# A streaming encoder layer on one core: down projections behind the next gate, reordered block products, low parts on GpSimd, modulation in smaller doses

## The chip, the cores and the metric

The kernel runs on one core of one Trainium2 chip. The metric is the time of one execution on the device, in microseconds (us); lower is better. Five engines work side by side, each through a queue of its own that it takes strictly in order: TensorE (PE, with its weight loads shown apart as PEld), VectorE (DVE), ScalarE (ACT), GpSimd (POOL) and SyncE (SP), which here issues the DMA transfers. Semaphores order work between engines.

## The reference

One layer of a streaming encoder for 1024 prompt frames and 32 sample frames, in fp32:

```python
def swiglu(h, w_gate, w_up, w_down):
    return (jax.nn.silu(h @ w_gate) * (h @ w_up)) @ w_down

mod = jax.nn.silu(c) @ w_mod + b_mod          # nine vectors: shift, scale, gate of three sub-layers
sh1, sc1, g1, sh2, sc2, g2, sh3, sc3, g3 = jnp.split(mod, N_MOD, axis=-1)
h = adaln_in(x, gains[0], sh1, sc1)
x = x + FFN_RES * g1[:, None] * rmsnorm(swiglu(h, w1_gate, w1_up, w1_down), gains[1])
h = adaln_in(x, gains[2], sh2, sc2)
...
x = x + g2[:, None] * rmsnorm(o, gains[3])
h = adaln_in(x, gains[4], sh3, sc3)
x = x + FFN_RES * g3[:, None] * rmsnorm(swiglu(h, w2_gate, w2_up, w2_down), gains[5])
```

The model width is 1024, the inner width of each SwiGLU (FFN1, FFN2) 2816. Between them stand one combined projection, two attention mixers and an output projection.

## The kernel before

The 1056 tokens are three blocks, `tb` 0, 1 and 2, of 384, 384 and 288. Each FFN goes through the 2816 inner columns in 11 groups of 256. A round of a group has three steps: gate "g" and up "u" (a 1024 x 256 weight matrix against the tokens), and down "d" (256 x 1024), whose result is added to an accumulator `facc` on VectorE (L802; the first round copies instead, L800). Which blocks a round has is set by `ROUNDS`: FFN1 has eight rounds with all blocks, then three with blocks 0 and 1, then three with block 2 alone; FFN2 has two rounds with blocks 0 and 1, two with block 2, then nine with all.

An fp32 operand is split into a high and a low part. `pair_of` does it for a weight tile `w` of 128x512: ScalarE copies the high part (L539), VectorE subtracts to get the low part (L540). A product then is three matmuls for each slice of 128: high x high, high x low, low x high (`product`, L597). So the first two matmuls need only the high part of the weight, the third the low part.

For blocks 0 and 1 gate and up use a Strassen scheme (`strassen`) of seven products. The weights enter as quarters A11 to A22 and as four sums S1 to S4, which GpSimd makes from the loaded tiles `raw` (`ws<-raw`, L563); the tokens enter as T1 to T4, combined once at the start of the FFN. The table `STRASSEN` sets the order of the products and, for each, the weights, the tokens, the PSUM bank, and whether block 2's plain product with the same quarter follows. The banks are added up on VectorE (L742) as they come; `made` then takes a finished quarter of the result: for gate, SiLU into `sl` on ScalarE; for up, `sl` times the result (L695) on VectorE, and the split of the product into `gg` (high part on ScalarE, L696, low part on VectorE, L697). The down step reads `gg`. PSUM tiles: `gu` holds banks "b" and "d", `ge` banks "a" and "e", `g2` (with `g` and `g_N` forms in the trace) block 2's. Round 0 of an FFN is done without Strassen (`plain`, tiles `gate` and `up`), and so are rounds with block 2 alone.

The list `stages` sets the program order of the steps: "g", "u", "d" of a round, except that among consecutive rounds of block 2 alone, the down step of one is held until behind the gate of the next. `load` and `ready` bring in the weights of the next step and make its first split while the present one runs.

Work that belongs to other parts runs beside the FFN in small steps: `step(n)` takes n steps from a list of generators. In FFN1 that is the modulation for the later sub-layers (`mod_aside`: chunks of three columns, 10 steps each: DMA loads `wma`, products with `csil` on VectorE into `macc`, L248 and L250, a transposition `pmt` on PE, L256, a sum, L257) and the rows of the attention bias. `step` is called with `PACE` = 2 after each Strassen product, with 1 after each pair of down tiles. At the end of the FFN the norm of the next sub-layer runs there: sums of squares `pss` on PE (L374) of `sq` from GpSimd (L387), `pr` (L422), and the normed tokens `h`, which the first projection `pv` reads (L934 to L936).

Weight buffers are few: four or five `raw` tiles, four `w` tiles, five tiles on GpSimd's side. Within a queue, the order of instructions is decided when the program is built: a scheduler with a timeline of its own may let an instruction pass others of its engine that wait.

Of the kernel before, what the change touches and what calls it, by code (L numbers as in the profile page):

```python
# [35 lines left out]
PACE = 2  # L36
# [45 lines left out]
def encoder_step(ctx: ExitStack, tc, x_prompt, x_sample, cache_a_k, cache_a_v, cache_b_k, cache_b_v,  # L82
# [453 lines left out]
    def pair_of(src, tag="w", at=None):  # L536

        w = at if at is not None else t_tile(tag, [128, 2, 4, 128], "w", F32R)
        ae.activation(w[:, 0], src, AF.Copy)  # L539
        ve.tensor_tensor(w[:, 1], src, w[:, 0], op=OP.subtract)  # L540
        return w[:, 0], w[:, 1]

    class Mat:
# [22 lines left out]
        def split(self, name):  # L566
            if name not in self.done:
                self.done[name] = pair_of(self.of(name), *(self.places.pop(0) if self.places else ()))
            return self.done[name]
# [68 lines left out]
    def rounds(key):  # L638
        lead, lag = ROUNDS[key]
        both, n, out = (0, 1, 2), NF // 2, []  # L640
        if lead:
# [5 lines left out]
    STRASSEN = [("A11", "B11", "a", 2), ("S2", "T2", "b", 0), ("S1", "T1", "d", 0), ("S3", "T3", "b", 0),  # L647
                ("A22", "T4", "e", 2), ("S4", "B22", "d", 0), ("A12", "B21", "a", 2), ("A21", None, None, 2)]

    def ffn(key, H, tags, F, facc, wg, wu, wd, per_group, key_out, after, beside=lambda: None):  # L650
# [3 lines left out]
        T, sl, gs, loaded = {}, {}, {}, {}  # L654
        stages = []
        for r, (gi, blocks) in enumerate(plan):
            held = [stages.pop()] if r and blocks == plan[r - 1][1] == (2,) else []
            stages += [(r, "g"), *held, (r, "u"), (r, "d")]
# [43 lines left out]
        def plain(r, what, m, tb, beside):  # L702
            w = TB[tb][1]
            names = [f"A{f + 1}{d + 1}" for f in range(2) for d in range(2)]
            for n, name in enumerate(names):
# [8 lines left out]
                if d == 1:  # L714
                    step(FAST if r == 0 else PACE)
                    made(r, what, f, tb, ps[:, :w])

        def strassen(r, what, m, two, beside):
# [26 lines left out]
            for n, (name, x, at, blk2) in enumerate(seq):  # L745
# [9 lines left out]
                if name == "A11":  # L755
                    ae.activation(temp("s", 1, 0), banks["a"], AF.Copy)
                elif name == "S2":
# [5 lines left out]
                elif name == "A22":  # L763
                    plus(v["s"], "e", "s")
                    made(r, what, 1, 0, v["s"])
                elif name == "S4":
                    plus(v["u"], "d", "u")
                    made(r, what, 0, 1, v["u"])
                elif name == "A12":
                    made(r, what, 0, 0, banks["a"])  # L770
                    if two:
                        made(r, what, 0, 2, banks["0"])
                elif name == "A21":
                    made(r, what, 1, 2, banks["1"])
                step(PACE)

# [36 lines left out]
        for i, (r, what) in enumerate(stages):  # L813
# [12 lines left out]
            if what == "d":  # L826
                for q in range(2):
                    m.split(q, 0)
                order = [tb for tb in (1, 0, 2) if tb in blocks]
# [796 lines left out]
```

## Time and profile before

| | us |
|---|---|
| three runs | 2378.19, 2384.40, 2382.83 |
| their median | 2382.83 |
| the profiled execution | 2381.55 |
| its span in the trace | 2379.7 |
| PE busy | 2158.8 (91%) |
| VectorE busy | 1583.0 (67%) |
| ScalarE busy | 849.1 (36%) |
| GpSimd busy | 440.5 (19%) |

The granted TensorE clock was 0.945 of full on average. The profile's page gives busy time by engine, the costliest groups of instructions by source line, and the DMA queues; the trace behind it can be asked for the waits of an engine, for groups in a window of time, and for the busy time of every engine in given windows. In the trace "out<-in" names what an instruction writes and reads, and L597 is line 597 of the kernel. "dn<-gg" are the down projections, "gu", "ge", "g" and "g2" the products of gate and up, "dn <- ACT gg" in a list of waits says that a down matmul waited for ScalarE's `gg`.

In time: 0 to 139 us the start with round 0 of FFN1; to 848 rounds 1 to 10; to 942 FFN1's last rounds (block 2 alone) and the change to the mixers; to 1513 projections, attention and output projection; to 1709 the first rounds of FFN2; to 2320 its nine full rounds but the last; to 2380 the end.

### The profile page before, as it was taken

The page shows a single profiled execution, that of the slowest core. Times are in us where ns is not written, and L with a number is a line of the kernel's source. Part 1 is how long each engine was busy: PE and PEld are TensorE (multiplying, and loading weights), DVE is VectorE, ACT ScalarE, POOL GpSimd, SP SyncE. Part 2 cuts the span into 40 slices and gives each one's busy share as a digit, 9 for nine tenths or more (in the row PEclk, how much of TensorE's full clock was granted, in tenths as well). Part 3 has the DMA queues.
Part 4 walks back from the last instruction along what each step waited for, and adds up shares of the span by engine and source line. Part 5 has one row for each costly group of instructions (what it writes and reads, how often), then busy time and mean ns, then how long its engine had stood idle before and what let it go on. Part 6 is the DMA issues. An engine that isn't in the chain of part 4 may idle for free.

```text
span 2379.7 us, 34693 instructions
## 1 busy us (share of the span) xinstructions
PE 2158.8 (91%) x13532; PEld 2036.6 (86%) x13532; DVE 1583.0 (67%) x3077; ACT 849.1 (36%) x1814; POOL 440.5 (19%) x449
## 2 busy tenths in 40 slices
PE   7898898799998896999999899948999999999998
PEld 4788798799998896988888589848999999999997
DVE  5899999965566588477544765776655545555548
ACT  4421222122222244367544662523322322222224
POOL 2321111110122023100100413332111102211101
PEclk8899999899999997999999899969999999999999
DMA  8233443331122254110211211311311111111104
GB/s 320 64 113 107 147 126 93 119 107 36 45 63 60 72 169 146 40 39 24 63 28 31 70 54 54 134 57 54 107 54 53 43 39 45 45 45 54 52 29 128
DMA packets 150840, 186.09 MB, mean 78 GB/s; under 512 B 7980, under 2 KB 134356, under 8 KB 149524
## 3 DMA queue, kind: packets, MB, share of 16 engines
q1 hardware_dynamic: 150676, 183.87, 24.8%
q8 instruction: 107, 1.75, 0.3%
q14 instruction: 57, 0.47, 0.1%
HBM read 164.12 MB, written 22.86 MB: 79 GB/s over the span
## 4 chain that ended last, share of the span: by engine, by line
PE 72%; DVE 19%; issue 3%; DMA 3%; ACT 1%; POOL 1%; SPq 0%; DVEq 0%; ACTq 0%; POOLq 0%
PE gu L597 11%; PE ge L597 8%; PE dn L795 6%; PE g L597 6%; PE dn L796 6%; PE dn L797 6%; DVE macc L250 4%; DVE w L540 3%; PE gate L597 3%; PE po L978 2%; PE S L1017 2%; PE pq L342 2%; DVE sl L695 2%; PE pq L344 2%; PE pq L343 2%
## 5 line engine op out<-in xcount | busy, mean ns | idle before, releaser
L795 PE MATMUL dn<-gg,w 128*128 128x384 f32 (+1 forms) x1008 | 344.7, 346 | 96.5 <-ACT gg L696 46.2
L539 ACT ACTIVATE w<-raw 128x512 fp32r<-128x512 f32 x298 | 186.1, 630 | 615.7 <-PE dn L797 226.4
L796 PE MATMUL dn<-gg,w 128*128 128x384 f32 (+1 forms) x1008 | 343.2, 341 | 11.1 <-DVE gg L697 11.1
L802 DVE TENSOR_TENSOR facc<-dn,facc 128x768 f32<-128x768 f32 (+1 forms) x240 | 212.8, 888 | 196.3 <-PE dn L797 194.8
L797 PE MATMUL dn<-gg,w 128*128 128x384 f32 (+1 forms) x1008 | 338.9, 336 | 0.0
L540 DVE TENSOR_TENSOR w<-raw,w 128x512 fp32r<-128x512 f32 x298 | 220.9, 745 | 161.3 <-ACT w L539 160.4
L795 PEld LDWEIGHTS dn<-gg,w 128*128 128x128 f32 x1008 | 199.5, 200 | 109.2 <-ACT gg L696 51.7
L563 POOL TENSOR_TENSOR ws<-raw 128x512 f32<-128x512 f32 x80 | 125.2, 1567 | 827.1 <-DMA raw<-in_w_gate_dram 266.5
L597 PE MATMUL gu<-t,w 128*128 128x384 f32 x1440 | 264.7, 335 | 0.0
L597 PEld LDWEIGHTS gu<-t,w 128*128 128x128 f32 x1440 | 248.6, 188 | 0.3 <-issue 0.2
L597 PE MATMUL g<-h_hi,w 128*128 128x288 f32 x1024 | 232.2, 300 | 18.1 <-DVE sl L695 9.7
L796 PEld LDWEIGHTS dn<-gg,w 128*128 128x128 f32 x1008 | 201.2, 200 | 17.6 <-DVE gg L697 17.4
L797 PEld LDWEIGHTS dn<-gg,w 128*128 128x128 f32 x1008 | 201.3, 200 | 0.0
L597 PEld LDWEIGHTS g<-h_hi,w 128*128 128x128 f32 x1024 | 175.9, 191 | 23.3 <-ACT w L539 12.0
L597 PE MATMUL ge<-h,w 128*128 128x384 f32 x960 | 194.4, 337 | 1.3 <-DVE w L540 0.9
L540 DVE TENSOR_TENSOR w<-ws,w 128x512 fp32r<-128x512 f32 x160 | 117.2, 739 | 82.8 <-ACT w L539 79.9
L539 ACT ACTIVATE w<-ws 128x512 fp32r<-128x512 f32 x160 | 98.9, 627 | 205.7 <-PE dn L797 117.8
L597 PEld LDWEIGHTS ge<-h,w 128*128 128x128 f32 x960 | 167.4, 188 | 1.9 <-DVE w L540 1.3
L250 DVE SCALAR_TENSOR_TENSOR macc<-wma,csil,macc 128x384 f32<-128x384 f32 (+1 forms) x266 | 165.1, 661 | 1.0 <-DMA wma<-in_w_mod_dram 1.0
L597 PE MATMUL g<-h_lo,w 128*128 128x288 f32 x512 | 152.5, 298 | 0.0
L597 PE MATMUL ge<-t,w 128*128 128x384 f32 x480 | 97.5, 341 | 7.3 <-DVE w L540 7.3
L597 PEld LDWEIGHTS g<-h_lo,w 128*128 128x128 f32 x512 | 97.4, 190 | 0.0
(294 smaller groups left out, 4342.0 us busy)
## 6 DMA issues: line engine op xcount, KB each, us to landing
raw<-in_w_gate_dram SPq DMA_DIRECT2D x54, 512.0 KB, 3.9
raw<-in_w_up_dram SPq DMA_DIRECT2D x54, 512.0 KB, 4.2
raw<-in_w_down_dram SPq DMA_DIRECT2D x54, 512.0 KB, 3.6
wma<-in_w_mod_dram SPq DMA_DIRECT2D x72, 384.0 KB, 3.6
raw<-in_w_in_dram SPq DMA_DIRECT2D x18, 512.0 KB, 4.7
raw<-in_w_out_dram SPq DMA_DIRECT2D x13, 512.0 KB, 3.7
wm<-in_w_mod_dram SPq DMA_DIRECT2D x8, 768.0 KB, 9.3
xr<-xs SPq DMA_DIRECT2D x16, 384.0 KB, 4.4
```

What stands on the lines that cost most here:

```text
L250: ve.scalar_tensor_tensor(acc[j], r[:, kk], c, acc[j], op0=OP.mult, op1=OP.add)
L342: te.matmul(ps, w[:, 0, k], hi, start=start, stop=False)
L343: te.matmul(ps, w[:, 0, k], lo, start=False, stop=False)
L344: te.matmul(ps, w[:, 1, k], hi, start=False, stop=stop)
L539: ae.activation(w[:, 0], src, AF.Copy)
L540: ve.tensor_tensor(w[:, 1], src, w[:, 0], op=OP.subtract)
L563: (ge if name in SUMS_POOL else ve).tensor_tensor(a[name], x, y, op=op)
L597: te.matmul(ps, w[a][:, k, :], x[b][k], start=first and k == 0 and q == 0, stop=last and k == n - 1 and q == 2, skip_group_check=True)
L795: te.matmul(ps[:, s, :w], h[:, k % 4, :], g[:, 0, :w], start=q == 0, stop=False)
L796: te.matmul(ps[:, s, :w], h[:, k % 4, :], g[:, 1, :w], start=False, stop=False)
L797: te.matmul(ps[:, s, :w], l[:, k % 4, :], g[:, 0, :w], start=False, stop=q == 1)
L802: ve.tensor_tensor(o, ps[:, :, :w], o, op=OP.add)
```

## The change

1. `PACE` is 1 in FFN1 and stays 2 in FFN2 (`pace`). In `plain`, `step` now stands behind `made` and is called after each product.
2. `pair_of` takes an engine: the low parts of S1 to S4 are made on GpSimd. 160 instructions leave VectorE for GpSimd; every other count of instructions stays.
3. The table `STRASSEN` has a new order: A12 comes second, S4 last. A down step works through the blocks in order 0, 1, 2 instead of 1, 0, 2. Both finished quarters of block 2 are taken after A21.
4. From round 1 on, every round's down step is held until behind the next round's gate, in all rounds and not just in those of block 2 alone. Only round 0's down and the last one follow their own up step.

Lines behind 568 move by one, behind 647 by two.

```diff
--- before.py
+++ after.py
@@ -33,7 +33,7 @@
              (16, 22, 26), (23, 31, 27), (32, 45, 28), (46, 63, 29), (64, 90, 30), (91, 127, 31)]
 
 
-PACE = 2
+PACE = 1
 FAST = 10
 OUTSTEP = 6
 ABREAST = 1
@@ -533,11 +533,11 @@
         yield from norm_h(f, tb, j + 1, H)
 
 
-    def pair_of(src, tag="w", at=None):
+    def pair_of(src, tag="w", at=None, by=None):
 
         w = at if at is not None else t_tile(tag, [128, 2, 4, 128], "w", F32R)
         ae.activation(w[:, 0], src, AF.Copy)
-        ve.tensor_tensor(w[:, 1], src, w[:, 0], op=OP.subtract)
+        (by or ve).tensor_tensor(w[:, 1], src, w[:, 0], op=OP.subtract)
         return w[:, 0], w[:, 1]
 
     class Mat:
@@ -565,7 +565,8 @@
 
         def split(self, name):
             if name not in self.done:
-                self.done[name] = pair_of(self.of(name), *(self.places.pop(0) if self.places else ()))
+                self.done[name] = pair_of(self.of(name), *(self.places.pop(0) if self.places else ()),
+                                          by=ge if name[0] == "S" else ve)
             return self.done[name]
 
     class Rows:
@@ -644,17 +645,18 @@
         out += [(g, (0, 1)) for g in range(n - lag, n)] + [(g, (2,)) for g in range(n - lag, n)]
         return out
 
-    STRASSEN = [("A11", "B11", "a", 2), ("S2", "T2", "b", 0), ("S1", "T1", "d", 0), ("S3", "T3", "b", 0),
-                ("A22", "T4", "e", 2), ("S4", "B22", "d", 0), ("A12", "B21", "a", 2), ("A21", None, None, 2)]
+    STRASSEN = [("A11", "B11", "a", 2), ("A12", "B21", "a", 2), ("S2", "T2", "b", 0), ("S1", "T1", "d", 0),
+                ("S3", "T3", "b", 0), ("A22", "T4", "e", 2), ("A21", None, None, 2), ("S4", "B22", "d", 0)]
 
     def ffn(key, H, tags, F, facc, wg, wu, wd, per_group, key_out, after, beside=lambda: None):
         plan = rounds(key)
         begun = set()
         final = {tb: max(i for i, (g, t) in enumerate(plan) if tb in t) for tb in range(3)}
         T, sl, gs, loaded = {}, {}, {}, {}
+        pace = PACE if key == "h1" else 2
         stages = []
         for r, (gi, blocks) in enumerate(plan):
-            held = [stages.pop()] if r and blocks == plan[r - 1][1] == (2,) else []
+            held = [stages.pop()] if r > 1 else []
             stages += [(r, "g"), *held, (r, "u"), (r, "d")]
 
         def load(i):
@@ -712,8 +714,8 @@
                 product(ps[:, :w], w_, half(tb, d), d == 0, d == 1)
                 beside(n)
                 if d == 1:
-                    step(FAST if r == 0 else PACE)
                     made(r, what, f, tb, ps[:, :w])
+                step((FAST if r == 0 else 3) if d else 2 * (r > 0))
 
         def strassen(r, what, m, two, beside):
             w, w2 = 384, TB[2][1]
@@ -754,6 +756,8 @@
                 beside(n)
                 if name == "A11":
                     ae.activation(temp("s", 1, 0), banks["a"], AF.Copy)
+                elif name == "A12":
+                    made(r, what, 0, 0, banks["a"])
                 elif name == "S2":
                     plus(temp("u", 0, 1), "b", "s")
                 elif name == "S3":
@@ -766,13 +770,10 @@
                 elif name == "S4":
                     plus(v["u"], "d", "u")
                     made(r, what, 0, 1, v["u"])
-                elif name == "A12":
-                    made(r, what, 0, 0, banks["a"])
-                    if two:
-                        made(r, what, 0, 2, banks["0"])
                 elif name == "A21":
+                    made(r, what, 0, 2, banks["0"])
                     made(r, what, 1, 2, banks["1"])
-                step(PACE)
+                step(pace)
 
         owns = {}
 
@@ -826,7 +827,7 @@
             if what == "d":
                 for q in range(2):
                     m.split(q, 0)
-                order = [tb for tb in (1, 0, 2) if tb in blocks]
+                order = list(blocks)
                 ending = any(r == final[tb] for tb in order)
                 todo = [(tb, mp) for tb in order for mp in range(4)] if ending else \
                     [(tb, mp) for h in range(2) for tb in order for mp in (2 * h, 2 * h + 1)]
```

Three places in the order of the queues. First PE in a steady group of FFN2, at the start of a down step. Before (`g2_17531` is block 2's product of the up step; `gg_17662` and `gg_17603` are the `gg` of this same up step):

```order
L597 MATMUL g2_17531<-h_hi_14934,w_17666 128x288 x2
L597 MATMUL g2_17531<-h_lo_14935,w_17666 128x288
L597 MATMUL g2_17531<-h_hi_14934,w_17666 128x288 x2
L597 MATMUL g2_17531<-h_lo_14935,w_17666 128x288
L597 MATMUL g2_17531<-h_hi_14934,w_17666 128x288
L795 MATMUL dn_17717<-gg_17662,w_17655 128x384
L795 MATMUL dn_17741<-gg_17662,w_17655 128x384
L796 MATMUL dn_17717<-gg_17662,w_17655 128x384
L797 MATMUL dn_17717<-gg_17662,w_17655 128x384
L795 MATMUL dn_17717<-gg_17603,w_17658 128x384
```

After (`gu_18366` is S4, the last product of the next round's gate; `gg_18156` and `gg_18252` were made in the previous round's up step, a whole gate step earlier):

```order
L598 MATMUL g2_18315<-h_hi_14938,w_18423 128x288 x2
L598 MATMUL g2_18315<-h_lo_14939,w_18423 128x288
L598 MATMUL g2_18315<-h_hi_14938,w_18423 128x288
L598 MATMUL gu_18366<-h_14562,w_18453 128x384 x12
L796 MATMUL dn_18486<-gg_18156,w_18413 128x384
L797 MATMUL dn_18486<-gg_18156,w_18413 128x384
L798 MATMUL dn_18486<-gg_18156,w_18413 128x384
L796 MATMUL dn_18486<-gg_18252,w_18416 128x384
```

The first down matmul used to stand right behind the up step that makes its `gg`; now a gate step stands between.

Second, GpSimd at the same stage. Before, its queue holds only sums, four for each gate or up step (each `ws` is one of S1 to S4, each pair of `raw` one weight matrix):

```order
L563 TENSOR_TENSOR ws_18021<-raw_17933,raw_17935 128x512
L563 TENSOR_TENSOR ws_18023<-ws_18021,raw_17933 128x512
L563 TENSOR_TENSOR ws_18025<-raw_17935,ws_18023 128x512
L563 TENSOR_TENSOR ws_18147<-raw_17933 128x512
L563 TENSOR_TENSOR ws_18446<-raw_18310,raw_18312 128x512
L563 TENSOR_TENSOR ws_18448<-ws_18446,raw_18310 128x512
L563 TENSOR_TENSOR ws_18450<-raw_18312,ws_18448 128x512
```

After (the `w` rows are low parts; `ws_18636` and the three behind it are the sums of the next up step, from the loads `raw_18500` and `raw_18502`; `w_18453` is the low part of S4 of the gate, which the PE rows above read):

```order
L540 TENSOR_TENSOR w_18334<-ws_18247,w_18334 128x512
L540 TENSOR_TENSOR w_18363<-ws_18245,w_18363 128x512
L540 TENSOR_TENSOR w_18383<-ws_18381,w_18383 128x512
L563 TENSOR_TENSOR ws_18636<-raw_18500,raw_18502 128x512
L563 TENSOR_TENSOR ws_18638<-ws_18636,raw_18500 128x512
L563 TENSOR_TENSOR ws_18640<-raw_18502,ws_18638 128x512
L563 TENSOR_TENSOR ws_18757<-raw_18500 128x512
L540 TENSOR_TENSOR w_18453<-ws_18249,w_18453 128x512
```

The low part `w_18453` stands behind the four sums of the next step, and the first of these waits for the DMA of its two `raw` tiles.

Third, PE at the end of FFN1 (`dn_8132` the last down tile of block 2, `pss_7617` and `pr_7722` the norm of block 0; `h_7743` is block 0's normed tokens). Before:

```order
L795 MATMUL dn_8132<-gg_8072,wd_8057 128x288
L796 MATMUL dn_8132<-gg_8072,wd_8057 128x288
L797 MATMUL dn_8132<-gg_8072,wd_8057 128x288
L374 MATMUL pss_7617<-ones_101,sq_7657 128x1 x3
L374 MATMUL pss_7617<-ones_101,sq_7683 128x1 x3
L422 MATMUL pr_7722<-ident_99,ry_7710 128x128 x3
L934 MATMUL pv_8213<-w_8172,h_7743 128x256
L935 MATMUL pv_8213<-w_8172,h_7743 128x256
L934 MATMUL pv_8268<-w_8172,h_7743 128x256
```

After (`h_7357` is block 0's):

```order
L796 MATMUL dn_8132<-gg_8072,wd_8057 128x288
L797 MATMUL dn_8132<-gg_8072,wd_8057 128x288
L798 MATMUL dn_8132<-gg_8072,wd_8057 128x288
L935 MATMUL pv_8213<-w_8172,h_7357 128x256
L935 MATMUL pv_8268<-w_8172,h_7357 128x256
L935 MATMUL pv_8301<-w_8172,h_7357 128x256
L936 MATMUL pv_8213<-w_8172,h_7357 128x256
L937 MATMUL pv_8213<-w_8172,h_7357 128x256
```

The rows of `pss` and `pr` that stood between the last down tile and the first `pv` are gone from there: block 0's norm is earlier in the queue, and that of block 1 stands some 30 rows behind the first `pv`.

## The prediction

> **What bounds the kernel now.** First the page: busy time by engine, and the costliest groups (operation, tiles, count | busy us, mean ns | idle just before, and what ended it).
>
> ```profile
> PE 2158.8 (91%) x13532; PEld 2036.6 (86%) x13532; DVE 1583.0 (67%) x3077; ACT 849.1 (36%) x1814; POOL 440.5 (19%) x449
> ...
> L540 DVE TENSOR_TENSOR w<-raw,w 128x512 fp32r<-128x512 f32 x298 | 220.9, 745 | 161.3 <-ACT w L539 160.4
> ...
> L563 POOL TENSOR_TENSOR ws<-raw 128x512 f32<-128x512 f32 x80 | 125.2, 1567 | 827.1 <-DMA raw<-in_w_gate_dram 266.5
> ...
> L540 DVE TENSOR_TENSOR w<-ws,w 128x512 fp32r<-128x512 f32 x160 | 117.2, 739 | 82.8 <-ACT w L539 79.9
> L539 ACT ACTIVATE w<-ws 128x512 fp32r<-128x512 f32 x160 | 98.9, 627 | 205.7 <-PE dn L797 117.8
> ```
>
> PE is busy 91% of the 2379.7 us span. The matmul count doesn't change, so what can be won is PE's idle time and the stretches at a lower clock: 221 us of span are not PE-busy. Second view, busy time by stage (columns: length, PE, PEld, DVE, ACT, POOL, granted clock, DMA share, GB/s):
>
> ```profile
> 139.00:848.00 709.00, 642.27 (x3811) 628.00 (x3810) 535.02 (x926) 179.66 (x327) 118.72 (x80) 0.96 0.30 91
> 848.00:942.00 94.00, 71.91 (x496) 70.07 (x495) 84.10 (x151) 47.07 (x76) 24.65 (x17) 0.85 0.55 174
> 942.00:1513.00 571.00, 552.70 (x3894) 478.70 (x3894) 349.04 (x998) 307.40 (x827) 100.15 (x210) 0.97 0.17 51
> 1513.00:1625.00 112.00, 69.01 (x353) 66.55 (x354) 85.67 (x162) 39.79 (x77) 40.74 (x30) 0.79 0.21 73
> 1709.00:2320.00 611.00, 585.56 (x3542) 576.47 (x3543) 327.86 (x464) 161.17 (x300) 105.31 (x71) 0.97 0.15 46
> ```
>
> 139–848 is FFN1 after its first round, 848–942 its end, 942–1513 projections and attention (untouched code), 1513–1709 the start of FFN2, 1709–2320 its steady groups. Third view, single groups: a group with modulation, one without, two rounds without block 2; then two FFN2 groups.
>
> ```profile
> 368.20:452.50 84.30, 74.20 (x432) 71.91 (x432) 78.79 (x146) 18.68 (x34) 12.62 (x9) 0.93 0.39 117
> 594.90:662.20 67.30, 65.78 (x408) 64.93 (x408) 37.54 (x55) 18.19 (x35) 11.54 (x8) 1.00 0.16 48
> 722.20:776.40 54.20, 47.64 (x264) 47.09 (x264) 32.10 (x45) 15.68 (x29) 11.90 (x8) 0.94 0.20 59
> 1756.87:1826.14 69.27, 66.04 (x408) 64.97 (x409) 38.36 (x55) 18.26 (x34) 12.20 (x9) 1.00 0.15 46
> 1826.14:1897.57 71.43, 68.36 (x408) 67.21 (x409) 38.49 (x55) 18.25 (x34) 12.20 (x9) 0.95 0.16 45
> ```
>
> The same group costs 67.3 or 84.3 us by whether VectorE carries modulation (78.8 of 84.3 us busy): early FFN1 is VectorE-bound, everything later PE-bound with short waits. Without waits a group would take 67.3 less the one 1.1 us wait left in it, 66.2 us. Fourth view, PE's waits in 139–848, in 848–942, in 1513–1709 and in 1709–2320 (total us, times, longest):
>
> ```profile
> PE dn L795 <- ACT gg L696: 28.1, 8, 6.6
> PE dn L795 <- DVE facc L802: 11.4, 10, 3.4
> PE dn L796 <- DVE gg L697: 8.8, 7, 2.2
> PE ge L597 <- DVE w L540: 8.3, 5, 2.6
> PE pmt L256 <- DVE modT L257: 5.5, 2, 2.8
> ```
> ```profile
> PE pss L374 <- POOL sq L387: 11.7, 2, 11.4
> PE pv L934 <- ACT h L469: 2.5, 1, 2.5
> PE pv L936 <- DVE h L471: 2.5, 1, 2.5
> PE pr L422 <- DVE ry L355: 2.3, 1, 2.3
> ```
> ```profile
> PE dn L795 <- DVE facc L800: 29.4, 3, 25.6
> PE dn L795 <- ACT gg L696: 9.1, 3, 5.6
> ```
> ```profile
> PE g L597 <- DVE sl L695: 9.7, 8, 1.2
> PE dn L795 <- ACT gg L696: 9.1, 8, 1.1
> PE g L597 <- DVE w L540: 5.8, 8, 0.7
> ```
>
> **The change, part by part.** All sums are made against the profiled execution, 2381.55 us, 1.3 us under the median of 2382.83; the terms are too coarse for that to matter.
>
> *Modulation spread out, FFN1 groups.* A full group issued 16 x 2 + 12 = 44 side steps, now 16 + 12 = 28. One modulation chunk is 10 steps. The rows of the group at 368.2 price it:
>
> ```profile
> L250 DVE SCALAR_TENSOR_TENSOR macc<-wma,csil,macc 128x384 f32<-128x384 f32 (+1 forms) x66 | 40.5, 652 | 0.2 <-DMA wma<-in_w_mod_dram 0.2
> L257 DVE TENSOR_REDUCE modT<-pmt 128x3 f32<-128x384 f32 x9 | 4.9, 546 | 0.0
> L248 DVE TENSOR_SCALAR macc<-wma,csil 128x384 f32<-128x384 f32 (+1 forms) x8 | 3.7, 502 | 0.3 <-DMA wma<-in_w_mod_dram 0.3
> ```
>
> Those 49.1 us and some 2 us of small coefficients over 4.4 chunks make 11.6 us a chunk, so 2.8 chunks bring 32.5 us instead of 51. VectorE's load in such a group is then 37.5 (the bare group) + 32.5 - 8 x 0.739 (the low parts gone) + 4.8 (what GpSimd's new work blocks, below) = 69 us against PE's 66.2: nearly balanced. Before, the period exceeded VectorE's load by 5.5 us; half of that gives 71 us. The 19 chunks and the 35 or so steps of the attention bias, some 225 in all, now reach into round 8 instead of round 5, so all six full groups (198.5 to 662.2, 463.7 us) cost 6 x 71 = 426: 38 saved. The rounds without block 2 lose their 6.6 us `gg` waits, because the down projection runs a round late: 28.1 us of `gg` less 10.6 of it inside the six groups is 17.5; I take 13, since the added steps of modulation stand there now. Round 1 gives 4. **Term: -55.** Bounds: groups at 75 and nothing else, -14; groups at 66.2 with all waits gone, -66 - 17 - 4 = -87.
>
> *Low parts on GpSimd.* 160 x 0.739 = 118 us leave VectorE. On GpSimd no such operation is in the trace; the nearest row is its own 128x512 sum, 1.567 us, so about 250 us more there, 690 of 2380 in all: no bound by load. What it costs VectorE shows in a timeline of 1963–1970 (start, duration):
>
> ```profile
> 1963.22 1.70 POOL L563 TENSOR_TENSOR ws<-raw 128x512 f32<-128x512 f32 x1 [28.94 <-DVE ut L742]
> ...
> 1963.69 1.64 DVE L695 TENSOR_TENSOR sl<-sl,ut 128x384 f32<-128x384 f32 x1
> 1965.00 1.49 POOL L563 TENSOR_TENSOR ws<-ws,raw 128x512 f32<-128x512 f32 x1
> 1965.26 0.54 DVE L742 TENSOR_TENSOR ut<-ge,ut 128x384 f32<-128x384 f32 x1
> 1965.73 0.54 DVE L695 TENSOR_TENSOR sl<-sl,ge 128x384 f32<-128x384 f32 x1
> ```
>
> An operation with both inputs in SBUF (`sl<-sl,ut`) took 1.64 us beside a GpSimd sum; those with one in PSUM kept 0.54. So one GpSimd operation costs VectorE between 0 and a whole 1.57 us; the one seen is 1.1. As VectorE often waits or reads PSUM, I take 0.6: 8 a group, the 4.8 above. The Trainium skill, "SBUF — State Buffer", section "Who interferes with whom", says that the loser of the shared port pair blocks for the other's whole instruction, which speaks against moving work between these two engines; the 1.64 us agree. By it alone the gain on VectorE would be negative (160 x 1.57 = 251 against 118): that is rival B.
>
> *Down behind the next gate, new product order, FFN2.* In each of eight steady groups PE waits 1.21 + 0.72 + 1.13 us (the last list above: 24.6 in all). All three have their cause in the end of the up step: its last results meet the four GpSimd sums and the activation of `gg`. Now `gg` is a round old when the down step reads it, and the last product of up is followed by a gate product on other banks. Those waits go. Six of eight groups also ran a stretch at a lower clock (granted 0.95 against 1.00, 71.43 against 69.27 us): 6 x 2.15 = 12.9. Full gain: 37.5 us. But what is late next: in the GpSimd queue the four sums of the next up stand ahead of the low part of the gate's S4. Worked from S2's start on PE: high part 0.63, low part of A22 on VectorE 0.74 (its end frees the raw buffer), load issued at 1.6, landed after 4.2 by this row,
>
> ```profile
> raw<-in_w_up_dram SPq DMA_DIRECT2D x54, 512.0 KB, 4.2
> ```
>
> four sums 6.3, the low part 1.57: ready at about 13.6. A group is 264 matmuls of 384 columns and 144 of 288, so the 65.78 us that PE was busy at clock 1.00 make 0.177 and 0.133 each; ahead of the matmul that needs the part stand 50 and 24, 12.0 us. New wait: 1.6 us, eight times, 12.8. **Term: -25**, bounds -37.5 and 0 (loads late by about 3 us).
>
> *FFN1's end.* Down now runs blocks 0, 1, so block 0's norm is ready first and `pv` of block 0 stands ahead of the sums of squares of block 1. Waits there: 11.7 + 2.5 + 2.5 + 2.3 = 19. VectorE is busy 84.1 of 94 us, so not all can go. **Term: -10**, bounds 0 and -15.
>
> *FFN2's start.* The 9.1 us of `gg` waits go; the 29.4 on `facc` is VectorE's own norm and combination work (85.7 us busy in 112) and stays. **Term: -9**, bounds 0 and -15. Round 0, 942–1513 and the end after 2320 keep their work: 0, give or take 3 each.
>
> Sum: -55 - 25 - 10 - 9 = -99, so **2283 us** (2282.6). All bounds at once: 2381.55 - 155 = 2227 and 2381.55 - 14 = 2368.
>
> **Rivals.**
>
> A. *The GpSimd queue takes back FFN2.* If loads land 3 us later than after 4.2, the wait on S4's low part is 4.6 us, and each of the eight groups gets the lower clock: -24.6 + 8 x 4.6 + 2 x 2.15 = +17 instead of -25, 2324 us. For: the order of the queue, in which one late load delays five operations. Against: a DMA share of only 0.15.
>
> B. *VectorE stays the bound of FFN1.* A full 1.57 us blocked for each moved part is 8 x (1.57 - 0.6) = 7.8 us more a group: 79 us periods, FFN1 -55 + 6 x 7.8 = -8, in all 2330. For: 1.64 against 0.54. Against: many of VectorE's operations there read PSUM.
>
> C. *No new wait.* VectorE's 69 us hide under PE, groups at 67.5 (FFN1 -76), FFN2 -37.5, the ends -12 and -10: 2246.
>
> D. *Slower.* GpSimd's low parts come late at each of 40 gate and up steps: a part that waits in the queue behind sums costs PE two GpSimd operations, 3.13 us, 40 x 3.13 = 125 against -99: 2408. It decides from 99 / 40 = 2.5 us a step. Against: S2, S1, S3 each have at least 12 matmuls (2.08 us) of A12 or A22 ahead as cover, and block 2's besides.
>
> E. *Within 0.3%*: B and A together with ends that give nothing.
>
> **How the numbers follow.** Forecast 0.48, A 0.14, B 0.14, C 0.11, D 0.08, E 0.05. A measurement here tells about 0.3% (7 us) from no change. The range takes in A, B and C with a few us of their own: 2235 to 2350; D, E and half a tenth of tails are left out. Faster: 0.48 + 0.14 + 0.14 + 0.11 = 0.87; same 0.05; slower 0.08.
>
> **What would show it.** Right: no `dn` wait on `gg` outside the first rounds; FFN1 groups of nearly equal length around 71 us with modulation until round 7 or 8; FFN2 groups at 67 to 69 us with one wait of 1 to 3 us on a GpSimd `w`; `pv` ahead of `pss` at 930. Wrong: `gu` waiting on GpSimd in FFN1 too, VectorE's 128x384 operations near 1.6 us throughout, or periods of 75 us and more.

## The result and the profile after

The changed kernel takes 2286.55 us (median of 4 runs, 2284.98 to 2292.99), the kernel before 2380.51 us beside it (4 runs): a ratio of 0.961, 95% interval 0.9584 to 0.9635, so 94 us less. The forecast was 2283.

The page of the changed kernel, busy time by engine and the groups that the change touches (lines behind 568 are one or two higher than before):

```profile
PE 2118.2 (93%) x13532; PEld 2003.9 (88%) x13532; DVE 1510.4 (66%) x2917; ACT 848.1 (37%) x1814; POOL 649.0 (28%) x609
...
L540 POOL TENSOR_TENSOR w<-ws,w 128x512 fp32r<-128x512 f32 x160 | 220.9, 1388 | 550.7 <-ACT w L539 547.4
L540 DVE TENSOR_TENSOR w<-raw,w 128x512 fp32r<-128x512 f32 x298 | 240.2, 815 | 193.2 <-ACT w L539 192.3
...
L563 POOL TENSOR_TENSOR ws<-raw 128x512 f32<-128x512 f32 x80 | 116.5, 1456 | 308.3 <-DVE macc L250 109.7
L250 DVE SCALAR_TENSOR_TENSOR macc<-wma,csil,macc 128x384 f32<-128x384 f32 (+1 forms) x266 | 183.6, 728 | 17.2 <-DMA wma<-in_w_mod_dram 17.1
...
raw<-in_w_up_dram SPq DMA_DIRECT2D x54, 512.0 KB, 3.8
```

160 low parts left VectorE, 118 us of work, yet VectorE is busy only 73 us less: the low parts of loaded weights that stayed grew from 745 to 815 ns each, and a modulation product takes 728 where its undisturbed time, as one of the versions below shows, is 600.

Where the time went, by rounds. A stage here runs from the first gate or up matmul of a round to that of another (counted by the number of L597/L598 matmuls, which is the same in all versions), on one profiled execution of each kernel, with spans of 2379.7 and 2284.0 us. Since the held down step moves a down step across these borders, the rounds at the ends are taken together:

| stage | before | after | difference | forecast |
|---|---|---|---|---|
| start and round 0 of FFN1 | 128.8 | 128.3 | -0.5 | 0 |
| FFN1 rounds 2 to 7 (all blocks) | 457.6 | 448.7 | -8.9 | -38 |
| FFN1 rounds 1 and 8 to 12 | 298.6 | 267.0 | -31.6 | -17 |
| FFN1 round 13, mixers | 628.7 | 623.9 | -4.8 | -10 |
| FFN2 rounds 5 to 11 | 497.8 | 463.5 | -34.4 | -22 |
| FFN2 rounds 0 to 4, 12 and the end | 368.2 | 352.7 | -15.5 | -12 |

The sum is -95.7 against -99 forecast, but the terms are not: FFN1's full groups gave a quarter of what was expected, FFN2 and the short rounds gave half as much again and more. The row of 628.7 is mostly code that did not change, and two versions below that keep the old end of FFN1 take 622.6 and 623.8 us there (low parts on GpSimd alone, thin modulation alone), so its 4.8 us are not shown to come from the change. The same two stretches in the windows view (length, PE, PEld, DVE, ACT, POOL busy, clock, DMA share, GB/s), FFN1 rounds 2 to 7 and FFN2 rounds 5 to 11, before:

```profile
219.30:676.90 457.60, 417.82 (x2535) 408.22 (x2535) 355.98 (x634) 110.49 (x204) 74.77 (x50) 0.97 0.31 93
1774.94:2272.77 497.83, 476.24 (x2857) 468.26 (x2857) 269.16 (x379) 127.77 (x238) 84.83 (x56) 0.96 0.15 45
```

and after:

```profile
194.96:643.64 448.68, 412.95 (x2547) 403.87 (x2546) 367.73 (x635) 110.71 (x204) 137.40 (x96) 0.99 0.33 99
1698.04:2161.49 463.45, 457.97 (x2857) 454.26 (x2857) 230.36 (x323) 128.82 (x238) 156.36 (x113) 1.00 0.16 48
```

In FFN2 the granted clock is 1.00 throughout and a group takes 66.2 us. In FFN1 a group still takes 74.8 us, with PE busy 68.8 and VectorE 61.3 of them: VectorE has less than the 69 forecast, and no engine is full. PE's waits in these two stretches, after (FFN1 first; each list whole down to 1.5 us in FFN1):

```profile
PE dn L796 <- DVE facc L803: 12.1, 12, 2.5
PE ge L598 <- DVE w L540: 5.1, 3, 2.5
PE dn L796 <- DVE sl L744: 5.1, 4, 1.8
PE gu L598 <- DVE ut L744: 4.4, 1, 4.4
PE dn L796 <- ACT sl L693: 2.6, 2, 1.3
PE gu L598 <- DVE facc L803: 2.6, 1, 2.6
PE g L598 <- DVE w L540: 1.6, 1, 1.6
PE g L598 <- DVE facc L803: 1.5, 1, 1.5
```
```profile
PE gu L598 <- POOL w L540: 4.4, 7, 1.7
PE g L598 <- DVE w L540: 0.7, 3, 0.3
```

The waits on `gg` are gone from both. In FFN2 the forecast new wait is there, on the low part from GpSimd, but it is 0.6 us on average and 1.7 only once. In FFN1 PE waits on VectorE in seven different places, for results that come late although VectorE has idle time. The queue of VectorE shows why. Ahead of the 2.5 us wait of `ge` on `w` that ends at 510.41 (start, duration):

```profile
505.95 0.63 ACT L539 ACTIVATE w<-raw 128x512 fp32r<-128x512 f32 x1
...
506.50 3.25 DVE L250 SCALAR_TENSOR_TENSOR macc<-wma,csil,macc 128x384 f32<-128x384 f32 x6
509.67 0.68 DVE L540 TENSOR_TENSOR w<-raw,w 128x512 fp32r<-128x512 f32 x1
```

The high part was done at 506.58; the low part started 3.1 us later, behind six modulation products. In 22 of the 23 waits on VectorE in these rounds (28.0 of 32.4 us) the awaited operation followed a modulation operation without idle time between them.

### The profile page after: what moved, and what is told of

It is laid out like the page before. It is cut to its first block, busy times and chain, and to the rows that moved or that the text cites. A ratio compares the mean times of both kernels' runs of the same rounds, so it can differ in the third digit from the quotient of the medians.

```text
span 2284.0 us, 34644 instructions
## 1 busy us (share of the span) xinstructions
PE 2118.2 (93%) x13532; PEld 2003.9 (88%) x13532; DVE 1510.4 (66%) x2917; ACT 848.1 (37%) x1814; POOL 649.0 (28%) x609
## 4 chain that ended last, share of the span: by engine, by line
PE 69%; DVE 16%; DMA 6%; POOL 4%; issue 2%; ACT 2%; SPq 0%; DVEq 0%; POOLq 0%; ACTq 0%
PE gu L598 9%; PE ge L598 8%; PE dn L796 6%; PE dn L797 6%; PE dn L798 6%; PE g L598 6%; DVE macc L250 5%; PE gate L598 3%; PE po L979 2%; POOL ws L563 2%; PE S L1018 2%; PE pq L342 2%; PE up L598 2%; DMA raw<-in_w_up_dram 2%; PE pq L344 2%
## 5 line engine op out<-in xcount | busy, mean ns | idle before, releaser
L796 PE MATMUL dn<-gg,w 128*128 128x384 f32 (+1 forms) x1008 | 333.2, 331 | 51.8 <-DVE facc L801 31.3
L540 POOL TENSOR_TENSOR w<-ws,w 128x512 fp32r<-128x512 f32 x160 | 220.9, 1388 | 550.7 <-ACT w L539 547.4
L540 DVE TENSOR_TENSOR w<-raw,w 128x512 fp32r<-128x512 f32 x298 | 240.2, 815 | 193.2 <-ACT w L539 192.3
L797 PE MATMUL dn<-gg,w 128*128 128x384 f32 (+1 forms) x1008 | 327.6, 325 | 0.0
L798 PE MATMUL dn<-gg,w 128*128 128x384 f32 (+1 forms) x1008 | 327.5, 325 | 0.0
L598 PE MATMUL gu<-t,w 128*128 128x384 f32 x1440 | 264.5, 335 | 3.4 <-DVE facc L803 2.6
L598 PEld LDWEIGHTS gu<-t,w 128*128 128x128 f32 x1440 | 248.4, 188 | 4.4 <-issue 3.1
L796 PEld LDWEIGHTS dn<-gg,w 128*128 128x128 f32 x1008 | 191.7, 190 | 60.2 <-DVE facc L801 32.4
L598 PE MATMUL g<-h_hi,w 128*128 128x288 f32 x1024 | 224.1, 296 | 5.0 <-DVE w L540 2.3
L563 POOL TENSOR_TENSOR ws<-raw 128x512 f32<-128x512 f32 x80 | 116.5, 1456 | 308.3 <-DVE macc L250 109.7
L250 DVE SCALAR_TENSOR_TENSOR macc<-wma,csil,macc 128x384 f32<-128x384 f32 (+1 forms) x266 | 183.6, 728 | 17.2 <-DMA wma<-in_w_mod_dram 17.1
L797 PEld LDWEIGHTS dn<-gg,w 128*128 128x128 f32 x1008 | 191.7, 190 | 0.0
L798 PEld LDWEIGHTS dn<-gg,w 128*128 128x128 f32 x1008 | 191.3, 190 | 0.0
L598 PE MATMUL ge<-h,w 128*128 128x384 f32 x960 | 185.7, 336 | 0.4 <-ACT w L539 0.4
L598 PEld LDWEIGHTS g<-h_hi,w 128*128 128x128 f32 x1024 | 171.4, 188 | 7.8 <-DVE w L540 4.7
L598 PEld LDWEIGHTS ge<-h,w 128*128 128x128 f32 x960 | 166.6, 188 | 0.8 <-ACT w L539 0.6
L598 PE MATMUL g<-h_lo,w 128*128 128x288 f32 x512 | 151.2, 295 | 0.0
L698 ACT ACTIVATE gg<-sl 128x384 fp32r<-128x384 f32 (+1 forms) x132 | 61.7, 492 | 144.9 <-DVE sl L697 144.3
L598 PE MATMUL ge<-t,w 128*128 128x384 f32 x480 | 99.0, 343 | 12.5 <-DVE w L540 8.7
```

Of the source, the lines that this page charges most:

```text
L250: ve.scalar_tensor_tensor(acc[j], r[:, kk], c, acc[j], op0=OP.mult, op1=OP.add)
L540: (by or ve).tensor_tensor(w[:, 1], src, w[:, 0], op=OP.subtract)
L563: (ge if name in SUMS_POOL else ve).tensor_tensor(a[name], x, y, op=op)
L598: te.matmul(ps, w[a][:, k, :], x[b][k], start=first and k == 0 and q == 0, stop=last and k == n - 1 and q == 2, skip_group_check=True)
L698: ae.activation(g[:, 0, :w], v, AF.Copy)
L796: te.matmul(ps[:, s, :w], h[:, k % 4, :], g[:, 0, :w], start=q == 0, stop=False)
```

## The experiments

Two theories to start with. The first is that of the prediction: FFN1's gain is that of the thinner modulation, FFN2's that of the held down step, and the low parts are near neutral. The rival gives the held down step both gains, and lets the low parts cost something. Each part is undone alone first.

**PACE back at 2.**

```diff
-PACE = 1
+PACE = 2
```

> The changed kernel with PACE back at 2 in FFN1, all else kept. Theory (spreading the modulation takes VectorE off the path of FFN1): the modulation is done by round 5 again, so groups of rounds 2 to 4 go back to about 80 us (44 steps instead of 28 bring 18 us more of VectorE work) and rounds 6 and 7 drop to 67 us; FFN1 is 15 to 40 us longer than in the changed kernel, FFN2 unchanged within 3 us. Rival (only where the modulation stands changes, not what it costs): rounds 2 to 7 sum to within 8 us of the changed kernel's 449 us.

Measured: 2302.38 us, 0.9688 of before (0.9672 to 0.9704), 16 us slower than the changed kernel. Rounds 2 to 7 take 461.4 us (79.7, 85.4, 85.7, 79.9, 65.4, 65.4) against 448.7; FFN2 is unchanged. The theory holds at its lower end: with the other parts in place, the pace is worth 16 us in all, and 12.7 in the six rounds where 38 were forecast.

**Low parts back on VectorE.**

```diff
-                                          by=ge if name[0] == "S" else ve)
+                                          by=ve)
```

> The changed kernel with the low parts of S1 to S4 back on VectorE, all else kept. Theory (near neutral: what VectorE gains by the 118 us it loses to blocking and to GpSimd's longer queue): total within 15 us of the changed kernel, FFN2 groups 66 us less the 0.6 us wait on GpSimd. Rival 1 (the low parts were what freed VectorE at the end of a step): FFN2 groups back at 68 us or more and FFN1 groups 5 us longer, total 45 us slower. Rival 2 (the shared-port blocking costs more than the move saves): FFN1 groups 3 us or more shorter, total 20 us faster.

Measured: 2266.49 us, 0.9528 (0.9514 to 0.9543): 20 us faster than the changed kernel. The theory (within 15 us) fails, and rival 2 comes true in the total, though the groups are 2.3 us shorter and not 3. The same two stretches of this kernel:

```profile
193.89:628.73 434.84, 411.97 (x2546) 402.96 (x2546) 376.75 (x683) 111.04 (x204) 73.69 (x48) 0.99 0.34 102
1680.97:2140.07 459.10, 456.32 (x2858) 454.09 (x2857) 261.27 (x379) 129.24 (x238) 84.94 (x56) 1.00 0.16 49
```

In rounds 2 to 7, 48 low parts more on VectorE raise its busy time by 9 us only (367.7 to 376.8), though by this kernel's row in that stretch they take 37:

```profile
L250 DVE SCALAR_TENSOR_TENSOR macc<-wma,csil,macc 128x384 f32<-128x384 f32 (+1 forms) x224 | 144.6, 682 | 4.4 <-DMA wma<-in_w_mod_dram 4.4
...
L540 DVE TENSOR_TENSOR w<-ws,w 128x512 fp32r<-128x512 f32 x49 | 37.3, 774 | 9.8 <-ACT w L539 9.7
...
L248 DVE TENSOR_SCALAR macc<-wma,csil 128x384 f32<-128x384 f32 (+1 forms) x32 | 11.8, 407 | 0.2 <-DMA wma<-in_w_mod_dram 0.2
L697 DVE TENSOR_TENSOR sl<-sl,ut 128x384 f32<-128x384 f32 x18 | 9.9, 549 | 0.0
```

With the low parts on GpSimd the same rows of the same stretch read:

```profile
L250 DVE SCALAR_TENSOR_TENSOR macc<-wma,csil,macc 128x384 f32<-128x384 f32 (+1 forms) x224 | 152.1, 717 | 10.1 <-DMA wma<-in_w_mod_dram 10.0
...
L248 DVE TENSOR_SCALAR macc<-wma,csil 128x384 f32<-128x384 f32 (+1 forms) x32 | 16.1, 539 | 0.0
...
L697 DVE TENSOR_TENSOR sl<-sl,ut 128x384 f32<-128x384 f32 x18 | 13.1, 728 | 0.1
```

Of the 37 us, 28 came back as longer operations on VectorE, 0.59 us for each of the 48. That is a figure of these rounds, where modulation keeps VectorE over 80% busy: in the whole kernel VectorE's busy time falls by 62.9 us (1573.3 to 1510.4) where low parts of 124.3 us moved, so about half came back. The group with the low parts on GpSimd is 2.3 us longer although VectorE has less to do and PE's busy time is the same (411.97 and 412.95): nearly all of it is PE waiting. It does not wait for GpSimd's low parts here (no row of its waits in these rounds names POOL), so the delay comes through VectorE, where a longer operation holds up what is queued behind it.

**Down step not held.**

```diff
-            held = [stages.pop()] if r > 1 else []
+            held = [stages.pop()] if r and blocks == plan[r - 1][1] == (2,) else []
```

> The changed kernel with every down step of rounds with all blocks directly behind its own up step again, new product order kept. Theory (the held down step is what removes the wait on gg): S4 is now the last product and its result needs two VectorE additions, a product and the activation before the first down matmul, so a wait of 3 to 6 us in every round; with the lower clock behind it FFN2's groups go from 66 to 71 to 74 us and FFN1's rounds grow by 4 us, total 60 to 100 us slower, at or above the kernel before. Rival (the order of the products alone moved the late results off the path): groups stay under 68 us.

Measured: 2347.93 us, 0.9871 (0.9847 to 0.9895), 61 us slower than the changed kernel. Its stretches and PE's waits in FFN2's seven groups:

```profile
217.07:697.05 479.98, 433.23 (x2540) 418.01 (x2538) 358.37 (x612) 109.56 (x204) 141.13 (x98) 0.93 0.31 93
1757.86:2237.39 479.53, 462.15 (x2857) 454.76 (x2857) 230.68 (x323) 128.33 (x238) 157.60 (x112) 1.00 0.16 47
```
```profile
PE gu L598 <- POOL w L540: 9.5, 7, 2.0
PE dn L796 <- ACT gg L698: 4.2, 7, 0.7
PE dn L796 <- DVE facc L803: 3.6, 6, 0.6
```

The total is as the theory has it, at its lower end. FFN2's groups take 68.5 us, not 71 to 74: waits return, but the lower clock does so in one of the seven groups only, for 3.4 us. FFN1's rounds 2 to 7 take 480.0 us, more than in the kernel before. The held step is by far the largest part, in FFN1 even more than in FFN2: 31 us of the 61 are in those six rounds, 16 in FFN2's seven groups. Of the 31, only 11 are added idle time of PE; 20 are PE's own busy time (412.95 to 433.23), at a granted clock of 0.93 instead of 0.99. So in FFN1 the lower clock did come back.

**Old table of products.** 

```diff
-    STRASSEN = [("A11", "B11", "a", 2), ("A12", "B21", "a", 2), ("S2", "T2", "b", 0), ("S1", "T1", "d", 0),
-                ("S3", "T3", "b", 0), ("A22", "T4", "e", 2), ("A21", None, None, 2), ("S4", "B22", "d", 0)]
+    STRASSEN = [("A11", "B11", "a", 2), ("S2", "T2", "b", 0), ("S1", "T1", "d", 0), ("S3", "T3", "b", 0),
+                ("A22", "T4", "e", 2), ("S4", "B22", "d", 0), ("A12", "B21", "a", 2), ("A21", None, None, 2)]
```

> The changed kernel with the old table of products (A12 and A21 last), down steps still held. Theory: the end of up no longer meets the down step, but the last plain product of block 2 still meets the next gate's product in the same pair of banks, so the waits of 1.2 and 0.7 us return, once or twice a group: FFN2 groups 68 to 70 us, with the lower clock 71; total 15 to 45 us slower. Rival (the held down step alone is the gain): groups within 0.7 us of 66.

Measured: 2294.43 us, 0.9648 (0.9633 to 0.9663), 8 us slower, with intervals that just touch. FFN2's groups are 66.1 us, as with the new table: the rival holds there. The last plain product no longer disturbs once the down step stands between up and the next gate. The 8 us are in FFN1, where rounds 2 to 7 take 457.8 us:

```profile
197.35:655.13 457.78, 422.51 (x2550) 409.69 (x2549) 375.20 (x634) 109.54 (x205) 139.55 (x97) 0.98 0.33 99
```

PE's busy time is 9.6 us longer there than in the changed kernel and its idle time the same, so with the old table PE does not wait more; it is busy longer, at a granted clock of 0.98 against 0.99. Why is open.

Now parts alone on the kernel before.

**Held down steps alone.** 

```diff
-            held = [stages.pop()] if r and blocks == plan[r - 1][1] == (2,) else []
+            held = [stages.pop()] if r > 1 else []
```

> The kernel before with the held down steps alone: every round's down step from round 1 on stands behind the next round's gate; old product order, old down order, PACE 2, low parts on VectorE. Theory (the held down step carries most of the gain, as its undoing cost 61 us): 45 to 70 us faster than before; FFN2's steady groups 66 to 67 us, the dn wait on gg gone; FFN1's rounds 2 to 4 still about 80 us. Rival (it needs the new order to work, since the last plain product still meets the next product in its banks): 25 us or less, FFN2 groups 68 us or more.

Measured: 2295.24 us, 0.9649 (0.9633 to 0.9665): 82 us of the 94 by this one line, more than the theory's 70. Its two stretches:

```profile
191.88:646.42 454.54, 421.45 (x2543) 410.58 (x2543) 365.41 (x671) 111.30 (x208) 71.78 (x49) 0.97 0.33 100
1712.80:2174.56 461.76, 456.72 (x2857) 454.49 (x2857) 253.69 (x379) 128.85 (x239) 79.60 (x56) 1.00 0.16 49
```

FFN2's groups are at 66.0 us and clock 1.00. The remaining waits in FFN1's rounds sit mostly on `facc` and `w`.

**Low parts on GpSimd alone.** 

```diff
-    def pair_of(src, tag="w", at=None):
+    def pair_of(src, tag="w", at=None, by=None):
...
-        ve.tensor_tensor(w[:, 1], src, w[:, 0], op=OP.subtract)
+        (by or ve).tensor_tensor(w[:, 1], src, w[:, 0], op=OP.subtract)
...
-                self.done[name] = pair_of(self.of(name), *(self.places.pop(0) if self.places else ()))
+                self.done[name] = pair_of(self.of(name), *(self.places.pop(0) if self.places else ()), by=ge if name[0] == "S" else ve)
```

> The kernel before with the low parts of S1 to S4 on GpSimd alone. Theory (the move costs what it cost in the changed kernel, by blocked VectorE operations and a longer way to the low part): 10 to 35 us slower than before, most of it in FFN1, VectorE's busy time falling by less than half of the 118 us moved. Rival (before the change the low part stood in VectorE's crowded queue, so there the move helps): 5 us or more faster.

Measured: 2390.12 us beside 2377.22, 1.0048 (1.0032 to 1.0064): 11 to 13 us slower, at the theory's lower end. Rounds 2 to 7 of FFN1 take 473.5 us against 457.6; FFN2's seven groups take 495.6 against 497.8, so the loss is in FFN1:

```profile
220.50:694.00 473.50, 425.09 (x2544) 414.15 (x2544) 344.02 (x583) 110.46 (x205) 141.01 (x99) 0.95 0.30 90
```

In the whole kernel VectorE's busy time falls by 76 us (1583.0 to 1506.9) where 118 moved; that is more than half, so this part of the expectation missed.

**Thin modulation alone.** On the kernel before, PACE 1 in FFN1 only:

```diff
-PACE = 2
+PACE = 1
...
+        pace = PACE if key == "h1" else 2
...
-                    step(FAST if r == 0 else PACE)
+                    step(FAST if r == 0 else 2)
...
-                step(PACE)
+                step(pace)
```

> The kernel before with PACE 1 in FFN1 alone (the FFN2 pace and everything else as before). Theory (the gain in FFN1 came from the held down step, and the spread modulation is a small part): 5 to 20 us faster; the longer rounds 2 to 4 shrink by 5 to 8 us each while rounds 5 to 7 grow. Rival (the step of the prediction: spreading takes VectorE off the path, worth 38 us in the six full groups by itself): 30 us or more faster.

Measured: 2381.42 us beside 2380.51, 1.0008 (0.9995 to 1.002): nothing. Rounds 2 to 7 take 78.8, 79.2, 83.1, 79.9, 77.6, 68.8 us instead of 85.0, 81.9, 87.2, 68.9, 67.4, 67.4: the later ones lose more than the early ones gain, and together they are 9.7 us longer (467.3 against 457.6) in this one execution. The mixers and the start of FFN2, which this edit does not touch, were as much shorter in it. PE's waits in FFN1's rounds (198 to 845 us), this kernel:

```profile
PE dn L796 <- ACT gg L697: 39.4, 9, 6.6
PE dn L797 <- DVE gg L698: 15.8, 7, 3.3
PE dn L796 <- DVE facc L803: 4.6, 9, 1.2
...
```

The kernel before waits 28.1 and 8.8 us on `gg` in the same window, so 18 us were added. As long as the down step reads `gg` fresh, rounds that carry modulation wait for it, and with the thin modulation more rounds carry some.

Last, versions that follow from the second experiment.

**Thinner still.** Low parts on VectorE, and in FFN1 no step after A12 and A21:

```diff
-                step(pace)
+                step(0 if key == "h1" and name in ("A12", "A21") else pace)
```

> The changed kernel with the low parts back on VectorE, and in FFN1 no side step after A12 and A21, so that a full group has 24 steps instead of 28 and the modulation lasts a round longer. Theory (each modulation operation in front of a needed one on VectorE costs, so thinner is better until it reaches the short rounds): rounds 2 to 7 lose 1 to 2 us each, rounds 8 and 9 gain up to 3; total 2 to 10 us faster than with the low parts on VectorE alone (2266.5), about 2260. Rival (total modulation work is what counts): within 2 us of it.

Measured: 2268.39 us, 0.9542 (0.9522 to 0.9562), the same as 2266.49: the rival holds. Rounds 2 to 7 gain 2.5 us in all, round 8 loses 8.

**Sums on VectorE too.** Low parts on VectorE, and

```diff
-SUMS_POOL = ("S1", "S2", "S3", "S4")
+SUMS_POOL = ()
```

> The changed kernel with low parts and also the sums S1 to S4 on VectorE, so that in the steady groups GpSimd does nothing. Theory (a GpSimd operation blocks VectorE for about as long as the same operation takes on VectorE): VectorE's modulation operations fall to 0.61 us each throughout, its busy time in rounds 2 to 7 changes by less than 10 us against 377 us although 48 sums of about 0.7 us come to it (33 us); FFN2 groups 65.4 to 66 us. Total within 15 us of 2266.5; slower if the sums, which wait for loads, hold up what is queued behind them on VectorE. Rival (blocking is small): VectorE's busy time there rises by 30 us or more.

Measured: 2250.42 us, 0.9465 (0.9447 to 0.9483): the fastest version, 36 us under the changed kernel and 16 under the one with only the low parts moved back. Its two stretches, in which GpSimd does nothing:

```profile
185.62:609.96 424.34, 409.10 (x2547) 400.26 (x2547) 373.22 (x733) 111.42 (x205) 0.00 (x0) 1.00 0.35 104
1676.08:2131.95 455.87, 455.72 (x2857) 454.13 (x2857) 274.87 (x435) 129.02 (x238) 0.00 (x0) 1.00 0.17 49
```

and VectorE's groups in the first:

```profile
L250 DVE SCALAR_TENSOR_TENSOR macc<-wma,csil,macc 128x384 f32<-128x384 f32 (+1 forms) x224 | 126.9, 600 | 4.3 <-DMA wma<-in_w_mod_dram 4.3
...
L540 DVE TENSOR_TENSOR w<-ws,w 128x512 fp32r<-128x512 f32 x49 | 33.0, 683 | 7.9 <-ACT w L539 7.9
...
L563 DVE TENSOR_TENSOR ws<-raw 128x512 f32<-128x512 f32 x24 | 16.4, 683 | 0.4 <-DVE modT L257 0.4
```

VectorE does 97 operations of 683 ns more there than in the changed kernel (66 us) and is busy 5.5 us more, as the theory has it; the total is a microsecond better than its range. A modulation product takes 600 ns on average, against 717 in the changed kernel. In FFN2 a group takes 65.1 us with PE busy all of it. There VectorE's busy time does rise with what it is given: 230.4 us in the changed kernel, 261.3 with the low parts, 274.9 with low parts and sums. Of the 16 us, the run does not tell apart what comes from shorter VectorE operations and what from sums that are ready earlier.

**The same with PACE 2.** On that version:

```diff
-PACE = 1
+PACE = 2
```

> The version with sums and low parts on VectorE, PACE back at 2. Theory: the spread modulation is worth about the 16 us that its undoing cost in the changed kernel, so 2260 to 2272. Rival (without GpSimd's blocking VectorE can take 44 steps a group beside PE): within 5 us of 2250.

Measured: 2269.46 us, 0.9534 (0.9519 to 0.9548): 19 us slower. The thin modulation is worth as much without GpSimd's blocking as with it, once the down step is held.

**The same with the old table.** On that version, with PACE 1, the edit of the table as in the fourth experiment.

> The version with sums and low parts on VectorE, with the old table of products. Theory (the new order's gain of 8 us does not hang on GpSimd): 2254 to 2264, FFN2 groups 65 to 66 us, the difference in FFN1. Rival (the new order only mattered where the low parts came late from GpSimd): within 3 us of 2250 or faster.

Measured: 2259.64 us, 0.9498 (0.9482 to 0.9513): 9 us slower, intervals touching again. Its two stretches:

```profile
186.14:617.10 430.96, 412.78 (x2548) 401.75 (x2547) 373.04 (x730) 110.64 (x204) 0.00 (x0) 1.00 0.35 104
1669.81:2134.14 464.33, 458.84 (x2858) 454.30 (x2857) 274.59 (x435) 128.31 (x238) 0.00 (x0) 1.00 0.16 48
```

FFN2's groups take 66.3 us instead of 65.1 and rounds 2 to 7 of FFN1 6.6 us more, so the theory holds in the total, but the difference is in FFN2 as much as in FFN1. The two profiled executions as a whole differ by 1.3 us only (spans 2255.3 and 2254.0), because other stages gave back what these two lost, 7.6 us of it in rounds 1 and 8 to 12 of FFN1.

## Why the prediction came out right, and where its steps failed

The total was right, and that it came within 4 us was luck: in the stages -8.9 stood against -38 forecast, and -31.6, -34.4 and -15.5 against -17, -22 and -12. The direction was not luck: the held down step, to which the forecast gave some 47 us (25 in FFN2's groups, 13 and 9 for waits on `gg` elsewhere), brings 82 by itself.

*Modulation spread out, -55.* The step that failed. FFN1's rounds 1 to 12 gained 40.5 us, but only 8.9 of it in rounds 2 to 7, where 38 were forecast from a period a little over VectorE's load. The load was read too high: the rows of the modulation were added up to 51 us, while the prediction's own groups with and without it differ by 41.3 (78.8 and 37.5 us busy): consecutive operations overlap, by 0.07 us in the prediction's own timeline, and adding rows counts that twice. With 41.3 the same sum gives about 63, and 61.3 was measured. That mistake helped, for a load below PE's 66.2 would have made the forecast shorter still, and the period was 74.8, with three of the six rounds above 75, which the prediction had named as a sign of being wrong. In these rounds it is not VectorE's load that sets the time but how late each single result is, behind modulation products in an in-order queue. Alone, the spread modulation moved nothing (1.0008); with the held step it is worth 16 to 19 us. The gain in FFN1 is that of the held step, which by itself brings FFN1's rounds 1 to 12 from 756.2 to 713.3 us with PACE 2, more than the whole change does (715.7).

*Low parts on GpSimd, 0.6 us blocked for each.* The size was a guess between 0 and 1.57, and it was right: 0.59 us in rounds 2 to 7. What failed is its place in the sum. Counted as load, the move was a small gain for VectorE (8 x 0.739 less, 4.8 more in a group); in the runs VectorE's load did fall, and the kernel still got 20 us slower. The Trainium skill, "SBUF — State Buffer", section "Who interferes with whom", says that a VectorE instruction with two inputs in SBUF contends with a GpSimd instruction that reads SBUF. The traces agree: in rounds 2 to 7 the modulation product, which has two, takes 717 ns beside sums and low parts on GpSimd, 682 beside the sums alone and 600 with GpSimd idle. Rival B's reading, each operation blocked for a whole one and groups of 79 us, is not borne out.

*Down behind the next gate, FFN2, -25.* Right in mechanism, too small: 34.4 us in seven groups, 4.9 each. All three waits went, and the lower clock went with them in all groups. The held step alone does it (66.0 us a group); the new product order adds nothing here as long as the sums are on GpSimd. The new wait on S4's low part exists where it was forecast but is 0.6 us, not 1.6. A timeline of GpSimd in one group of the changed kernel shows why (start, duration):

```profile
1910.20 1.29 POOL L563 TENSOR_TENSOR ws<-raw 128x512 f32<-128x512 f32 x1 [7.04 <-DMA raw<-in_w_up_dram]
1911.57 1.62 POOL L563 TENSOR_TENSOR ws<-ws,raw 128x512 f32<-128x512 f32 x1
1913.27 1.28 POOL L563 TENSOR_TENSOR ws<-raw,ws 128x512 f32<-128x512 f32 x1
1914.51 1.74 POOL L563 TENSOR_TENSOR ws<-raw 128x512 f32<-128x512 f32 x1
1916.21 1.28 POOL L540 TENSOR_TENSOR w<-ws,w 128x512 fp32r<-128x512 f32 x1
```

The queue stood as read, sums first and the low part last, but a GpSimd operation that nothing holds up takes 1.28 us, not the mean of 1.57 that was used; the five took 7.3 us instead of 7.9, and the loads landed after 3.8 us instead of 4.2. Rival A, which needed later loads, did not occur.

*The ends, -10 and -9.* FFN1's end with the mixers gave 4.8, which is within what this stage varies. `pv` of block 0 starts earlier as forecast and the 11.7 us on `sq` are gone from its front, but a new wait stands behind it, for the low part of the projection's own weights, at 892 us:

```profile
PE pv L936 <- DVE w L337: 7.3, 1, 7.3
```

FFN2's start and end gave 15.5 us; if the eighth group gained 4.9 as the others did, some 10.6 are left where 9 were forecast. The new order of blocks in the down step and the moved steps in `plain` were not tried by themselves, so what they add stays open, as does the reason for the order's 8 us. Of the 31.6 us in rounds 1 and 8 to 12, 17.5 are idle time of PE, as forecast; the other 14 are PE's busy time, which was not forecast, at a clock of 0.97 and 0.99 instead of 0.92 and 0.95 and with 43 matmuls fewer between these borders.

## What to carry to other kernels

Look first for a step that reads what the step before has just made: putting one independent step between them (one line here) gave 82 of 94 us, on the part with the modulation as well as on the part where the wait was only 1.1 us. The parts of a change are not additive: the thin modulation was worth nothing while the fresh `gg` was read and 16 to 19 us afterwards. Before moving elementwise work from VectorE to GpSimd, compare the durations of VectorE's operations with two SBUF inputs beside a GpSimd operation and alone; here the move cost 20 us, and moving the rest the other way gained another 16. A load below that of the busiest engine does not say that a queue is out of the way: look at what stands ahead of the awaited operation.

## What the hardware showed unexpectedly

The same 128x512 operation on two SBUF inputs takes 1.28 us on an undisturbed GpSimd and 0.68 on VectorE, but beside modulation VectorE's own time hardly changed with who does it: 367.7, 376.8 and 373.2 us in rounds 2 to 7 with 0, 49 and 97 of these operations on VectorE. In FFN2, without modulation, it did change: 230.4, 261.3 and 274.9 us with 0, 56 and 112.

In FFN2 of the kernel before, the lower clock stood behind waits far shorter than the time that it lasted. From about a microsecond after waits of 1.2 and 0.7 us the granted clock was 0.50 for 6.8 us, in six of the eight groups; in the other two the same waits left it at 1.00. One stretch of that kernel, and the only one in the seven groups of the version with the down step not held:

```profile
1828.00:1834.80 6.80, 5.67 (x20) 5.04 (x19) 4.13 (x9) 2.12 (x5) 1.19 (x1) 0.50 0.79 226
```
```profile
2221.40:2224.80 3.40, 3.16 (x10) 2.66 (x10) 2.43 (x6) 1.88 (x5) 0.19 (x1) 0.50 0.60 166
```

In that version waits of 1.0 to 2.0, 0.7 and 0.6 us stood within 9 us in each of the other six groups, and the clock stayed at 1.00. What decides between the two is not shown.
